# Gated delta rule in a hybrid backbone: k first, q and v loaded behind the block inverse's way to scratch, decayed queries made one step ahead

## The chip, the cores and the metric

One Trainium2 chip, one of its cores. The metric is the device time of one execution in microseconds (us); the median of the executions counts. A whole two-layer network runs in one program, and the change touches one of its stages, which occurs once in each layer.

## What is computed

The network has two layers; each is a feed-forward block, a token mixer, and a second feed-forward block, on 256 context and 256 latent tokens of width 1024. The mixer has four branches (a state space scan, an mLSTM, an S5 scan and a gated delta rule, GDN), whose outputs are gated and merged. The change is in the GDN branch. Cut to what matters (4 heads, keys and values of 128, run forward and backward over the tokens; the kernel uses chunks of 128 tokens where the reference has 64):

```python
def gdn_scan(q, k, v, lg, beta, s0):
    g = cumsum(lg) within a chunk
    lmat = (k*beta) k^T * exp(masked_diff(g, strict))
    tmat = triangular_solve(eye + lmat, eye)          # the inverse
    u_base, w_k = tmat (v*beta), tmat (k*beta*exp(g))
    a_qk = q k^T * exp(masked_diff(g))
    q_dec = q * exp(g)                                # decayed queries
    step: u = u_base - w_k s;  o = q_dec s + a_qk u;  s = exp(g_last) s + k_dec^T u
```

Before it q, k and v pass a short convolution and SiLU, and q and k are normalized to unit length. In layer 0 all four chunks give outputs; in layer 1 only the two latent ones do (`o0 = 2` skips q and the outputs of the others).

## The kernel before

**Order of the work.** `Backbone.mix` (L1817) walks a list of words written out by hand, `MIX_ORDER` (L1752), one string for each layer. A word like `ga2` is a projection of the gates (a pair of weight chunks, 2 x 24 matmuls); `gdn:1` runs the generator `Gdn.gdn` to its next `yield`, `gdn:6` six yields; `glu`, `zG0`, `m1` are other projections; `out` takes the GDN result through its norm, and `m0` to `m3` merge the branches. The order of words is a priority: the scheduler of the language orders each engine's instructions at build time by its own model of times, and an instruction that it holds ready early goes ahead of earlier words. `"!"` in front of a word queues its instructions behind the latest projection's last matmul on PE, weight cast on ACT, weight split on DVE and weight load on SP; `"'"` behind the last matmul alone. The queue of each engine is then fixed, and each engine works it in order.

**Projections.** `weights` (L360) loads a 512 KB chunk on the SP queue (L365), casts it on ACT (L366) and splits off the low part on DVE (L371); `proj` (L384) runs three matmuls for each product (L380 to L382). Three chunks are buffered (`nwf = 3`, L35). Small tiles (`k2`) come from a ring of 11 buffers (L33), big ones (`t8`) from ten numbered places.

**GDN** (L1234 on), by yields: (1) `to_tok` for k: four loads L1246, transposes L1249, copy L1250, squares L1253 and their sums L1254; (2) the same for v; (3) for q, then one `rsqrt` over both sums (L264 to L270), the normalization (L1267) and the transposes back (L1270, L1271); (4 to 7) for each chunk c the products k k^T (L1288) and k q^T (L1292), the decay E for both directions (loaded over all partitions, L1295; ACT L1298 for the forward one, GpSimd L1300 for the backward one, exponential L1301), the entries of the inverse's matrix LT on DVE (L1303), and the attention weights (L1306 on GpSimd, L1307 on DVE). Then `inverse`: the 32 x 32 diagonal blocks go to scratch in DRAM, one for each partition (BD L1134 and L1135, eight stores `gl` L1141, one load L1147), are solved by 31 substitution steps (L1158, L1160, columns below 12 on DVE and the rest on GpSimd), and come back (store `gz` L1162, eight loads L1168, transposes L1169); matmuls L1194 to L1225 double the blocks to 64 and 128. Four steps of the recurrence follow (L1321 to L1362); each makes its decayed queries in place (load L1350, exponential L1351, product L1352) ahead of the matmuls L1356.

Of the kernel before, what the change touches and what calls it, by code (L numbers as in the profile page):

```python
# [562 lines left out]
ORDER = ((0, 1, 2, 3), (1, 0, 3, 2))  # L563
# [555 lines left out]


class Gdn:
    def inverse(self, LT):


        nc = self.nc
        pt_ = nc.gpsimd.tensor_tensor
        sub = lambda: [self.k2([128, 16, 32]) for _ in range(2)]
        dma = nc.sync.dma_start
        TT = [self.t8(5, [128, 16, 128]), None]

        BD = sub()
        for b in range(4):
            q = slice(32 * b, 32 * b + 32)
            nc.vector.transpose(BD[0][q], LT[0][q, :, q])  # L1134
            nc.scalar.copy(BD[1][q], LT[1][q, :, q])  # L1135
        dl = self.dp.tile([128, 32, 32], F32, tag="gl", name=self.nm("gl"), bufs=1)
        dz = self.dp.tile([128, 32, 32], F32, tag="gz", name=self.nm("gz"), bufs=1)
        dv = lambda t, b, d: t[b * 32 + d * 16:b * 32 + d * 16 + 16].rearrange("u r c -> r u c")
        for b in range(4):
            for d in range(2):  # L1140
                dma(dv(dl, b, d), BD[d][32 * b:32 * b + 32])  # L1141
        LZ = self.t8(6, [128, 2, 32, 32])
        Lo, Z = LZ[:, 0], LZ[:, 1]
        nc.gpsimd.memset(Z, 0.0)
        nc.gpsimd.memset(Z.rearrange("p a b -> p (a b)")[:, ::33], 1.0)
        nc.gpsimd.memset(TT[0], 0.0)
        dma(Lo, dl)  # L1147
        yield
        for j in range(31):
            n = 31 - j  # L1150
# [8 lines left out]
                   Z[:, j, c0:c1].unsqueeze(1).to_broadcast([128, n, m]), op=OP.mult)  # L1159
                op(Z[:, j + 1:, c0:c1], Z[:, j + 1:, c0:c1], pr, op=OP.subtract)  # L1160
        yield
        dma(dz, Z)  # L1162
        TT[1] = self.t8(6, [128, 16, 128])
        nc.gpsimd.memset(TT[1], 0.0)
        ZB, ZT = sub(), sub()
        for d in range(2):
            for b in range(4):
                dma(ZB[d][32 * b:32 * b + 32], dv(dz, b, d))  # L1168
            nc.vector.transpose(ZT[d], ZB[d])  # L1169
        X = lambda d: (ZB if d == 0 else ZT)[d]  # L1170
        XT = lambda d: (ZT if d == 0 else ZB)[d]
# [3 lines left out]
        for d in range(2):  # L1175
            for b in range(4):
                q = slice(32 * b, 32 * b + 32)
# [27 lines left out]
        for d, a, qa, qb, _ in half:  # L1205

            pt = self.ps()
# [13 lines left out]
        for two in (quart[:2], quart[2:]):  # L1221
            pt = [self.ps() for _ in two]
# [11 lines left out]
    def gdn(self, l, P, G, o0):  # L1234
        nc, A = self.nc, self.A
        W = A["w_in"][l]
        t0 = o0 * 128
        tt, ts, stt = nc.vector.tensor_tensor, nc.vector.tensor_scalar, nc.vector.scalar_tensor_tensor

        kt, vt, qt = (self.t8(i, [128, 4, 4, 128]) for i in (4, 7, 6))  # L1240
        ss = self.keep("gss", [128, 2, 4, 4])

        def to_tok(j0, dst, c0, sums):
            for c in range(c0, 4):
                src = self.k2([128, 4, 128])
                nc.sync.dma_start(src, self.dG[j0:j0 + 4, :, c * 128:(c + 1) * 128].rearrange("h p t -> p h t"))  # L1246
                pt = self.ps()
                for h in range(4):
                    nc.tensor.transpose(pt[:, h * 128:(h + 1) * 128], src[:, h], self.ident)  # L1249
                nc.scalar.copy(dst[:, c].rearrange("p h e -> p (h e)"), pt)  # L1250
                if sums is not None:
                    sq = self.k2([128, 4, 128])
                    nc.scalar.activation(sq, dst[:, c], AF.Square)  # L1253
                    nc.vector.tensor_reduce(sums[:, c], sq, axis=mybir.AxisListType.X, op=OP.add)  # L1254
        to_tok(4, kt, 0, ss[:, 0])
        yield
        to_tok(8, vt, 0, None)
        yield
        if o0:
            nc.gpsimd.memset(ss[:, 1, 0:o0], 1.0)  # L1260
        to_tok(0, qt, o0, ss[:, 1])
        self.rsqrt(ss, ss, 1.0)
        ts(ss[:, 1], ss[:, 1], 128 ** -0.5, None, op0=OP.mult)
        kT, qT = self.t8(3), self.t8(0)
        for t, T_, sums, c0 in ((kt, kT, ss[:, 0], 0), (qt, qT, ss[:, 1], o0)):
            for c in range(c0, 4):
                tt(t[:, c], t[:, c], sums[:, c].unsqueeze(2).to_broadcast([128, 4, 128]), op=OP.mult)  # L1267
                pt = self.ps()
                for h in range(4):
                    nc.tensor.transpose(pt[:, h * 128:(h + 1) * 128], t[:, c, h], self.ident)  # L1270
                nc.scalar.copy(T_[:, :, c * 128:(c + 1) * 128], pt.rearrange("p (h t) -> p h t", h=4))  # L1271
        rv = self.rowd[16:24].rearrange("(d h) t -> d h t", d=2)
        b4 = lambda ap: ap.unsqueeze(2).to_broadcast([128, 4, 128])
        hv = lambda p: p.rearrange("p (h v) -> p h v", h=4)
# [5 lines left out]

        at = [self.t8(8 + i, [128, 4, 4, 128]) for i in range(2 - l)]
        own = lambda c, d: at[(c - o0) // 2][:, c % 2 * 2 + d]
        for c in range(4):
            yield
            sl = slice(c * 128, (c + 1) * 128)
            pg, pa = self.ps(), None
            for h in range(4):
                nc.tensor.matmul(pg[:, h * 128:(h + 1) * 128], lhsT=kT[:, h, sl], rhs=kT[:, h, sl], start=True, stop=True)  # L1288
            if c >= o0:
                pa = self.ps()  # L1290
                for h in range(4):
                    nc.tensor.matmul(hv(pa)[:, h], lhsT=kT[:, h, sl], rhs=qT[:, h, sl], start=True, stop=True)  # L1292
            for d in range(2):
                E = self.k2([128, 4, 128])
                nc.sync.dma_start(E, rv[d, :, c * 128:(c + 1) * 128].partition_broadcast(128))  # L1295
                for h in range(4):
                    if d == 0:
                        nc.scalar.activation(E[:, h], E[:, h], AF.Relu, scale=-1.0, bias=G8("g", c, d, h))  # L1298
                    else:
                        nc.gpsimd.tensor_scalar(E[:, h], E[:, h], G8("g", c, d, h), 0.0, op0=OP.subtract, op1=OP.min)  # L1300
                nc.scalar.activation(E, E, AF.Exp, scale=(-1.0, 1.0)[d])  # L1301
                for h in range(4):
                    stt(LT[d][:, c * 4 + h], pg[:, h * 128:(h + 1) * 128], G["beta"][:, c, d, h:h + 1], E[:, h],  # L1303
                        op0=OP.mult, op1=OP.mult)
                if pa is not None:
                    nc.gpsimd.tensor_tensor(own(c, d), E, self.tri[:, d].unsqueeze(1).to_broadcast([128, 4, 128]), op=OP.mult)  # L1306
                    tt(own(c, d), own(c, d), hv(pa), op=OP.mult)  # L1307
        TT = yield from self.inverse(LT)
        yield
        oT, gS = self.t8(1), self.t8(2)  # L1310
        S, seen = [None, None], set()
        for i in range(4):
            cs = [ORDER[d][i] for d in range(2)]
            sl = [slice(c * 128, (c + 1) * 128) for c in cs]
            both = range(2)
# [28 lines left out]
            for d in both:  # L1344
                c = cs[d]
                if c < o0:
                    continue
                if i:
                    gb = self.k2([128, 4, 128])
                    nc.sync.dma_start(gb, rv[d, :, c * 128:(c + 1) * 128].partition_broadcast(128))  # L1350
                    nc.scalar.activation(gb, gb, AF.Exp)  # L1351
                    nc.gpsimd.tensor_tensor(gb, gb, qT[:, :, sl[d]], op=OP.mult)  # L1352
# [34 lines left out]
class S5:  # L1387
# [364 lines left out]
MIX_ORDER = (  # L1752
# [7 lines left out]
)  # L1760


# [245 lines left out]
```

## Time and profile before

| | us |
|---|---|
| median of 3 runs | 2816.64 (2812.92 to 2817.88) |
| the profiled execution's own time | 2805.0 |
| its span, first to last instruction | 2803.3 |
| TensorE busy | 2687.4 (96%) |
| VectorE busy | 1729.0 (62%) |
| mean granted TensorE clock | 0.979 of full speed |

Times below are positions in the profiled span. The GDN stage of layer 0 lies between 877 and 1123 us, that of layer 1 between 2343 and 2560 us. Engines: PE is TensorE, DVE VectorE, ACT ScalarE, POOL GpSimd, SP the queue that issues the DMAs.

### The profile page before, as it was taken

What the parts mean: (1) busy time and instruction counts of PE and PEld (TensorE: products, weight loads), DVE (VectorE), ACT (ScalarE), POOL (GpSimd) and SP (SyncE); (2) the same over time, 40 slices, a digit from 0 to 9 for tenths busy, and PEclk for the clock granted to TensorE, in tenths of its full rate; (3) what the DMA queues carried; (4) which work ended last, traced back from release to release, by engine and by line L of the source; (5) the groups of instructions that cost most, each with busy time, mean ns of one, the idle gap of its engine ahead of it and who ended that gap; (6) DMA issues with size and microseconds to landing.
All of it is one profiled execution on the core that took longest, in us unless ns stands there. A gap on an engine that the chain in (4) does not pass through costs nothing.

```text
span 2803.3 us, 46292 instructions
## 1 busy us (share of the span) xinstructions
PE 2687.4 (96%) x17710; PEld 2258.2 (81%) x17710; DVE 1729.0 (62%) x3234; ACT 1114.1 (40%) x1711; POOL 748.3 (27%) x1129
## 2 busy tenths in 40 slices
PE   7999999999999998999999999999998999969999
PEld 5777669787878778897678897777987888969999
DVE  6654436578975575674333476654464997776665
ACT  4322224445464542252212353323354556623544
POOL 1433001394030322520000024330016951434100
PEclk9999999999999999999999999999999999979999
DMA  8444887755475562567662364444476558753564
GB/s 267 127 156 123 266 278 225 172 165 159 143 214 172 147 202 92 196 209 258 228 232 91 98 167 122 134 131 127 132 201 188 160 186 252 223 164 118 178 195 151
DMA packets 509820, 494.18 MB, mean 176 GB/s; under 512 B 79381, under 2 KB 437839, under 8 KB 508575
## 3 DMA queue, kind: packets, MB, share of 16 engines
q1 hardware_dynamic: 509598, 491.22, 57.6%
q8 instruction: 140, 2.29, 0.3%
q14 instruction: 82, 0.66, 0.1%
HBM read 429.17 MB, written 61.96 MB: 175 GB/s over the span
## 4 chain that ended last, share of the span: by engine, by line
PE 50%; DVE 9%; issue 4%; DMA 4%; POOL 2%; ACT 1%; SPq 1%; DVEq 0%; POOLq 0%; ACTq 0%
PE ffn.pb L380 11%; PE ffn.pb L381 11%; PE ffn.pb L382 11%; PE gates.pb L380 2%; PE gates.pb L381 2%; PE gates.pb L382 2%; PE ffn.ps L187 1%; PE merge.pb L382 1%; PE merge.pb L380 1%; PE merge.pb L381 1%; DVE gdnin.kf L790 1%; PE wout.pb L382 1%; PE wout.pb L381 1%; PE wout.pb L380 1%; DVE ssmin.kf L790 1%
## 5 line engine op out<-in xcount | busy, mean ns | idle before, releaser
L371 DVE TENSOR_TENSOR ffn.wl<-ffn.wf,ffn.wh 128x1024 fp32r<-128x1024 f32 (+1 forms) x308 | 369.3, 1199 | 373.1 <-ACT ffn.wh L366 363.6
L366 ACT CAST ffn.wh<-ffn.wf 128x1024 fp32r<-128x1024 f32 (+1 forms) x308 | 310.7, 1009 | 550.9 <-PE ffn.pb L382 388.3
L382 PE MATMUL ffn.pb<-ffn.t,ffn.wh 128*128 128x256 f32 (+1 forms) x1312 | 437.5, 336 | 0.0
L381 PE MATMUL ffn.pb<-ffn.t,ffn.wl 128*128 128x256 f32 (+1 forms) x1312 | 437.3, 335 | 0.0
L380 PE MATMUL ffn.pb<-ffn.t,ffn.wh 128*128 128x256 f32 (+1 forms) x1312 | 433.7, 337 | 1.0 <-ACT ffn.t L344 1.0
L380 PEld LDWEIGHTS ffn.pb<-ffn.t,ffn.wh 128*128 128x128 f32 x1312 | 243.4, 188 | 34.2 <-ACT ffn.wh L366 4.2
L382 PEld LDWEIGHTS ffn.pb<-ffn.t,ffn.wh 128*128 128x128 f32 x1312 | 246.3, 188 | 30.0 <-issue 2.4
L381 PEld LDWEIGHTS ffn.pb<-ffn.t,ffn.wl 128*128 128x128 f32 x1312 | 247.2, 188 | 28.3 <-issue 1.6
L380 PE MATMUL ffn.pb<-wout.t,ffn.wh 128*128 128x256 f32 (+1 forms) x720 | 240.8, 336 | 1.0 <-ACT wout.t L344 1.0
L381 PE MATMUL ffn.pb<-wout.t,ffn.wl 128*128 128x256 f32 (+1 forms) x720 | 239.6, 333 | 0.0
L382 PE MATMUL ffn.pb<-wout.t,ffn.wh 128*128 128x256 f32 (+1 forms) x720 | 237.3, 332 | 0.0
L381 PE MATMUL gates.pb<-ffn.t,gates.wl 128*128 128x512 f32 (+1 forms) x512 | 176.7, 346 | 5.4 <-DVE gates.wl L371 5.4
L313 POOL TENSOR_TENSOR norm.kf<-norm.kf,norm.kf 128x256 f32<-128x256 f32 x45 | 43.0, 956 | 518.0 <-ACT norm.kf L311 517.3
L380 PE MATMUL gates.pb<-ffn.t,gates.wh 128*128 128x512 f32 (+1 forms) x512 | 175.2, 344 | 0.6 <-ACT zs.kf L807 0.6
L382 PE MATMUL gates.pb<-ffn.t,gates.wh 128*128 128x512 f32 (+1 forms) x512 | 175.8, 344 | 0.0
L380 PEld LDWEIGHTS ffn.pb<-wout.t,ffn.wh 128*128 128x128 f32 x720 | 135.9, 189 | 26.6 <-ACT ffn.wh L366 7.5
L381 PEld LDWEIGHTS ffn.pb<-wout.t,ffn.wl 128*128 128x128 f32 x720 | 136.1, 189 | 16.2 <-DVE ffn.kf L498 0.8
L382 PEld LDWEIGHTS ffn.pb<-wout.t,ffn.wh 128*128 128x128 f32 x720 | 134.9, 188 | 15.9 <-issue 0.8
L380 PE MATMUL ffn.pb<-t,ffn.wh 128*128 128x512 f32 x352 | 141.9, 404 | 2.0 <-DVE ffn.kf L493 1.9
L381 PE MATMUL ffn.pb<-t,ffn.wl 128*128 128x512 f32 x352 | 142.3, 405 | 0.0
L382 PE MATMUL ffn.pb<-t,ffn.wh 128*128 128x512 f32 x352 | 138.9, 400 | 0.0
L493 DVE SCALAR_TENSOR_TENSOR ffn.kf<-ffn.kf,ffn.pb 128x512 f32<-128x512 f32 (+1 forms) x88 | 54.6, 620 | 94.8 <-ACT ffn.kf L491 94.8
(583 smaller groups left out, 6321.0 us busy)
## 6 DMA issues: line engine op xcount, KB each, us to landing
ffn.wf<-in_ffn_up_dram SPq DMA_DIRECT2D x176, 512.0 KB
ffn.t<-in_ada_w_dram SPq DMA_DIRECT2D x68, 1024.0 KB
ffn.wf<-in_ffn_down_dram SPq DMA_DIRECT2D x104, 512.0 KB
gates.wf<-in_w_in_dram SPq DMA_DIRECT2D x64, 512.0 KB
merge.wf<-in_w_branch_dram SPq DMA_DIRECT2D x32, 512.0 KB
zs.wf<-in_w_in_dram SPq DMA_DIRECT2D x24, 512.0 KB
gdnin.wf<-in_w_in_dram SPq DMA_DIRECT2D x24, 512.0 KB
wout.wf<-in_w_out_dram SPq DMA_DIRECT2D x24, 512.0 KB
```

Of the source, the lines that this page charges most:

```text
L187: nc.tensor.matmul(pm[32 * k:32 * k + 32, :], lhsT=self.sF[:, h * 4 + k, 28 - 4 * i:60 - 4 * i], rhs=ws[h][:, k], start=(h == 0), stop=(h ...
L313: nc.gpsimd.tensor_tensor(sq[0], sq[0], q, op=OP.add)
L366: self.w_cast = nc.scalar.copy(wh[:, :nk, :nw], wf[:, :nk, :nw])
L371: self.w_split = nc.vector.tensor_tensor(wl[:, :nk, :nw], wf[:, :nk, :nw], wh[:, :nk, :nw].bitcast(F32), op=OP.subtract)
L380: mm(out, lhsT=ah, rhs=bh, start=start, stop=False)
L381: mm(out, lhsT=al, rhs=bh, start=False, stop=False)
L382: self.last_mm = mm(out, lhsT=ah, rhs=bl, start=False, stop=stop)
L493: nc.vector.scalar_tensor_tensor(g[:, :n], t[:, :n], 1.0, p, op0=OP.add, op1=OP.mult)
L790: nc.vector.scalar_tensor_tensor(av, tap(k), cw[:, k:k + 1], av, op0=OP.mult, op1=OP.add)
```

## The change

K is loaded and normalized first, by itself. The decay rows are loaded one chunk ahead, and the backward decay is made on DVE rather than on GpSimd. The diagonal blocks go to scratch in two parts (the first 12 of the 16 chunk-head pairs after chunk 2, the last four after chunk 3), each part with one DMA for each direction over all 128 partitions, in a scratch laid out as direction, pair, row. Q is loaded and normalized behind the blocks' way to scratch, and the attention weights are finished there; v is loaded behind the substitution and transposed (`values`) while the blocks come back, which takes two loads instead of eight. The inverse's tile is in place 7 instead of 6, where v comes later. The decayed queries are made one step ahead. The words of `MIX_ORDER` are respaced. The core of the diff, with `...` for what is left out:

```diff
-    def inverse(self, LT):
+    def inverse(self, LT, values):
...
+        for u in (slice(0, 12), slice(12, 16)):
+            for b in range(4):
+                q = slice(32 * b, 32 * b + 32)
+                nc.vector.transpose(BD[0][q, u], LT[0][q, u, q])
+                nc.scalar.copy(BD[1][q, u], LT[1][q, u, q])
             for d in range(2):
-                dma(dv(dl, b, d), BD[d][32 * b:32 * b + 32])
-        LZ = self.t8(6, [128, 2, 32, 32])
+                dma(dl[d, u].rearrange("u q c -> q u c"), BD[d][:, u])
+            if u.start == 0:
+                yield
+        LZ = self.t8(7, [128, 2, 32, 32])
...
         for d in range(2):
-            for b in range(4):
-                dma(ZB[d][32 * b:32 * b + 32], dv(dz, b, d))
+            dma(ZB[d], dz[d].rearrange("u q c -> q u c"))
+        values()
+        for d in range(2):
             nc.vector.transpose(ZT[d], ZB[d])
...
-        to_tok(4, kt, 0, ss[:, 0])
-        yield
-        to_tok(8, vt, 0, None)
-        yield
...
+        def normalized(t, T_, sums, c0):
+            self.rsqrt(sums[:, c0:], sums[:, c0:], 1.0, 0)
...
+        src = load(4, 0)
+        yield
+        to_tok(src, kt, 0, ss[:, 0])
+        yield
+        kT = self.t8(3)
+        normalized(kt, kT, ss[:, 0], 0)
...
+        Es = rows(0)
         for c in range(4):
             yield
...
+            Ec, Es = Es, rows(c + 1) if c < 3 else None
...
-                        nc.gpsimd.tensor_scalar(E[:, h], E[:, h], G8("g", c, d, h), 0.0, op0=OP.subtract, op1=OP.min)
+                        ts(E[:, h], E[:, h], G8("g", c, d, h), 0.0, op0=OP.subtract, op1=OP.min)
...
+            if c > 1:
+                next(inv)
+        src = load(0, o0)
+        yield
+        qt, qT = self.t8(6, [128, 4, 4, 128]), self.t8(0)
+        to_tok(src, qt, o0, ss[:, 1])
+        normalized(qt, qT, ss[:, 1], o0)
...
+        yield
+        next(inv)
+        v["src"] = load(8, 0)
+        yield
+        TT = yield from inv
...
         for i in range(4):
+            for d in range(2) if i < 3 else ():
+                c = ORDER[d][i + 1]
+                if c >= o0:
+                    gb = gbs[i + 1, d] = self.k2([128, 4, 128])
+                    nc.sync.dma_start(gb, rv[d, :, c * 128:(c + 1) * 128].partition_broadcast(128))
+                    nc.scalar.activation(gb, gb, AF.Exp)
+                    nc.gpsimd.tensor_tensor(gb, gb, qT[:, :, c * 128:(c + 1) * 128], op=OP.mult)
...
-    "!s5:1 ga2 's5:1 gb2 s5:1 gdn:1 gc2 gdn:1 gd2 gdn:6 ga0 glu gb0 gc0 gd0 zG0 zG2 !gdn:1 ga3 gb3 'gdn:6 gc3 gd3 "
-    "out m1 m2 m3 m0",
+    "!s5:1 ga2 's5:1 gb2 s5:1 gdn:1 gc2 gdn:1 glu gdn:2 gd2 gdn:1 ga0 gdn:1 gb0 gdn:1 gc0 gdn:1 gd0 !gdn:1 zG0 zG2 "
+    "ga3 gb3 !gdn:1 gc3 'gdn:6 gd3 out m1 m2 m3 m0",
...
-    "'ssm:1 i4 !ssm:1 i6 !ssm:1 i8 !ssm:1 i10 !ssm:1 i0 !ssm:1 !s5:1 i2 's5:1 zG0 s5:1 zG2 gdn:1 ga2 gdn:1 gb2 gdn:6 "
-    "gc2 glu gd2 ga1 gb1 gc1 gd1 ga0 gb0 gc0 gd0 !gdn:1 ga3 gb3 'gdn:6 gc3 gd3 out m2 m1 m3 m0",
+    "'ssm:1 i4 !ssm:1 i6 !ssm:1 i8 !ssm:1 i10 !ssm:1 i0 !ssm:1 !s5:1 i2 's5:1 zG0 s5:1 zG2 gdn:1 ga2 gdn:1 gb2 glu "
+    "gdn:2 gc2 gdn:1 gd2 gdn:1 ga1 gdn:1 gb1 gdn:1 gc1 gd1 !gdn:1 ga0 gb0 gc0 gd0 ga3 gb3 !gdn:1 gc3 'gdn:6 gd3 out "
+    "m2 m1 m3 m0",
```

## Rows read from the trace of the kernel before

**Rows 1.** The page: busy us, share of the span, instructions; then 40 slices in tenths.
```profile
PE 2687.4 (96%) x17710; PEld 2258.2 (81%) x17710; DVE 1729.0 (62%) x3234; ACT 1114.1 (40%) x1711; POOL 748.3 (27%) x1129
...
PE   7999999999999998999999999999998999969999
```

**Rows 2.** Stretches: length, busy us (xcount) of PE, PEld, DVE, ACT, POOL; clock, DMA.
```profile
2343.00:2482.40 139.40, 127.08 (x1062) 124.27 (x1061) 109.09 (x218) 84.59 (x143) 48.41 (x65) 0.98 0.84 246
2482.40:2498.80 16.40, 0.00 (x0) 0.00 (x0) 11.07 (x32) 1.04 (x1) 6.62 (x6) 0.56 0.56 175
2498.80:2524.20 25.40, 22.51 (x448) 22.01 (x448) 10.71 (x22) 8.46 (x14) 5.11 (x7) 0.54 0.12 19
2524.20:2559.80 35.60, 31.91 (x259) 31.06 (x257) 18.61 (x54) 7.58 (x15) 10.01 (x9) 0.95 0.16 45
877.80:975.90 98.10, 94.43 (x464) 77.31 (x462) 52.51 (x78) 51.91 (x87) 26.82 (x27) 1.00 0.58 172
```

**Rows 3.** Timeline of PE, layer 1: start, us, instruction, [idle before <- what ended it].
```profile
2377.62 0.55 PE L1249 MATMUL gdn.ps<-ident,gdn.k 128*128 128x128 f32 x3 [1.20 <-DMA gdn.k<-ffn.gdn]
...
2427.54 0.58 PE L381 MATMUL gates.pb<-ffn.t,gates.wl 128*128 128x256 f32 x1 [4.08 <-DVE gates.wl L371]
...
2454.37 0.28 PE L380 MATMUL merge.pb<-ffn.t,merge.wh 128*128 128x256 f32 x1
...
2498.83 1.38 PE L1194 MATMUL gdn.ps<-gdn.k,gdn.t 32*32 32x32 f32 x22 [16.46 <-DMA gdn.k<-gdn.gz]
...
2504.79 3.27 PE L1194 MATMUL gdn.ps<-gdn.k,gdn.t 32*32 32x32 f32 x61 [2.53 <-DVE gdn.k L1169]
...
2552.62 1.95 PE L283 MATMUL gdn.ps<-ones,gdn.k 128*128 128x1 f32 x16 [1.29 <-ACT gdn.k L839]
2556.57 3.47 PE L300 MATMUL gdn.ps<-ident,gdn.rstd 128*128 128x128 f32 x16 [2.00 <-POOL gdn.rstd L258]
```

**Rows 4.** Timeline of DVE, layer 1, from k's last sum to the end of the substitution.
```profile
2372.64 0.69 DVE L1254 TENSOR_REDUCE gdn.gss<-gdn.k 128x4 f32<-128x512 f32 x1
...
2390.98 0.18 DVE L264 TENSOR_SCALAR gdn.rsq<-gdn.gss 128x32 f32<-128x32 f32 x1
...
2425.08 1.27 DVE L1307 TENSOR_TENSOR gdn.t<-gdn.t,gdn.ps 128x512 f32<-128x512 f32 x2
...
2442.87 0.21 DVE L1158 TENSOR_TENSOR gdn.gpr<-gdn.t 128x31 f32<-128x31 f32 x1 [1.95 <-DMA gdn.t<-gdn.gl]
...
2494.05 0.17 DVE L1160 TENSOR_TENSOR gdn.t<-gdn.t,gdn.gpr 128x12 f32<-128x12 f32 x1
```

**Rows 5.** Timeline of the SP queue, layer 1: the GDN's loads among others.
```profile
2371.84 4.69 SPq L1246 DMA_DIRECT2D gdn.k<-ffn.gdn  x5
...
2388.78 7.67 SPq L1295 DMA_DIRECT2D gdn.k<-rows.rowd  x8
...
2435.97 0.47 SPq L1147 DMA_DIRECT2D gdn.t<-gdn.gl  x1
```

**Rows 6.** Groups, layer 1: xcount | busy us, mean ns of one | idle before <- releasers.
```profile
L1300 POOL TENSOR_SCALAR gdn.k<-gdn.k,rows.gc 128x128 f32<-128x128 f32 x16 | 16.8, 1068 | 54.8 <-ACT gdn.k L1298 54.8
...
L371 DVE TENSOR_TENSOR merge.wl<-merge.wf,merge.wh 128x1024 fp32r<-128x1024 f32 x9 | 12.1, 1346 | 1.7 <-ACT merge.wh L366 1.7
L818 DVE TENSOR_SCALAR gates.kf<-gates.kf 128x256 f32<-128x256 f32 x30 | 11.8, 396 | 7.5 <-ACT gates.kf L817 7.5
...
L1160 DVE TENSOR_TENSOR gdn.t<-gdn.t,gdn.gpr 128x192 f32<-128x192 f32 (+16 forms) x18 | 7.0, 389 | 0.2
```

**Rows 7.** Timelines of PE and ACT, layer 0.
```profile
975.89 2.08 PE L1288 MATMUL gdn.ps<-gdn.t 128*128 128x128 f32 x8 [2.61 <-DVE gdn.t L1303]
...
1051.72 2.01 PE L1194 MATMUL gdn.ps<-gdn.k,gdn.t 32*32 32x32 f32 x61
...
1110.76 0.63 ACT L1351 ACTIVATE gdn.k<-gdn.k 128x512 f32<-128x512 f32 x1 [5.95 <-DMA gdn.k<-rows.rowd]
...
1112.78 0.80 PE L1356 MATMUL gdn.ps<-gdn.k,gdn.t 128*128 128x128 f32 x2 [4.44 <-POOL gdn.k L1352]
```

More of the change, by code (lines that the diff above doesn't have):

```diff
@@ L1128, in inverse @@
         dma = nc.sync.dma_start
-        TT = [self.t8(5, [128, 16, 128]), None]
+        dl, dz = (self.dp.tile([2, 16, 128, 32], F32, tag=n, name=self.nm(n), bufs=1) for n in ("gl", "gz"))
         BD = sub()
-        for b in range(4):
[L1133 to L1139, printed above, removed]
+        for u in (slice(0, 12), slice(12, 16)):
[3 more added lines that the diff above has]
+                nc.scalar.copy(BD[1][q, u], LT[1][q, u, q])
             for d in range(2):
-                dma(dv(dl, b, d), BD[d][32 * b:32 * b + 32])
-        LZ = self.t8(6, [128, 2, 32, 32])
+                dma(dl[d, u].rearrange("u q c -> q u c"), BD[d][:, u])
+            if u.start == 0:
+                yield
+        LZ = self.t8(7, [128, 2, 32, 32])
         Lo, Z = LZ[:, 0], LZ[:, 1]
@@ L1145, in inverse @@
         nc.gpsimd.memset(Z.rearrange("p a b -> p (a b)")[:, ::33], 1.0)
+        TT = [self.t8(5, [128, 16, 128]), None]
         nc.gpsimd.memset(TT[0], 0.0)
-        dma(Lo, dl)
+        dma(Lo, dl.rearrange("d u (b r) c -> (d u b) r c", b=4))
         yield
@@ L1161, in inverse @@
         yield
-        dma(dz, Z)
+        dma(dz.rearrange("d u (b r) c -> (d u b) r c", b=4), Z)
         TT[1] = self.t8(6, [128, 16, 128])
@@ L1166, in inverse @@
         for d in range(2):
-            for b in range(4):
-                dma(ZB[d][32 * b:32 * b + 32], dv(dz, b, d))
+            dma(ZB[d], dz[d].rearrange("u q c -> q u c"))
+        values()
+        for d in range(2):
             nc.vector.transpose(ZT[d], ZB[d])
@@ L1238, in gdn, with load, to_tok @@
         tt, ts, stt = nc.vector.tensor_tensor, nc.vector.tensor_scalar, nc.vector.scalar_tensor_tensor
-        kt, vt, qt = (self.t8(i, [128, 4, 4, 128]) for i in (4, 7, 6))
+        kt = self.t8(4, [128, 4, 4, 128])
         ss = self.keep("gss", [128, 2, 4, 4])
[L1243 to L1246, printed above, removed]
+        def load(j0, c0):
+            src = [self.k2([128, 4, 128]) for _ in range(c0, 4)]
+            for s, c in zip(src, range(c0, 4)):
+                nc.sync.dma_start(s, self.dG[j0:j0 + 4, :, c * 128:(c + 1) * 128].rearrange("h p t -> p h t"))
+            return src
+        def to_tok(src, dst, c0, sums):
+            for s, c in zip(src, range(c0, 4)):
                 pt = self.ps()
                 for h in range(4):
-                    nc.tensor.transpose(pt[:, h * 128:(h + 1) * 128], src[:, h], self.ident)
+                    nc.tensor.transpose(pt[:, h * 128:(h + 1) * 128], s[:, h], self.ident)
                 nc.scalar.copy(dst[:, c].rearrange("p h e -> p (h e)"), pt)
@@ L1254, in to_tok @@
                     nc.vector.tensor_reduce(sums[:, c], sq, axis=mybir.AxisListType.X, op=OP.add)
-        to_tok(4, kt, 0, ss[:, 0])
-        yield
-        to_tok(8, vt, 0, None)
-        yield
[L1259 to L1265, printed above, removed]
+        def normalized(t, T_, sums, c0):
+            self.rsqrt(sums[:, c0:], sums[:, c0:], 1.0, 0)
+            if t is not kt:
+                ts(sums[:, c0:], sums[:, c0:], 128 ** -0.5, None, op0=OP.mult)
             for c in range(c0, 4):
@@ L1282, in gdn, with values, rows @@
         own = lambda c, d: at[(c - o0) // 2][:, c % 2 * 2 + d]
+        v = {}
+        def values():
+            v["t"] = self.t8(7, [128, 4, 4, 128])
+            to_tok(v["src"], v["t"], 0, None)
+        inv = self.inverse(LT, values)
+        def rows(c):
+            E = [self.k2([128, 4, 128]) for _ in range(2)]
+            for d in range(2):
+                nc.sync.dma_start(E[d], rv[d, :, c * 128:(c + 1) * 128].partition_broadcast(128))
+            return E
+        Es = rows(0)
         for c in range(4):
@@ L1285, in gdn @@
             sl = slice(c * 128, (c + 1) * 128)
-            pg, pa = self.ps(), None
+            pg = self.ps()
             for h in range(4):
                 nc.tensor.matmul(pg[:, h * 128:(h + 1) * 128], lhsT=kT[:, h, sl], rhs=kT[:, h, sl], start=True, stop=True)
[L1289 to L1292, printed above, removed]
+            Ec, Es = Es, rows(c + 1) if c < 3 else None
             for d in range(2):
-                E = self.k2([128, 4, 128])
-                nc.sync.dma_start(E, rv[d, :, c * 128:(c + 1) * 128].partition_broadcast(128))
+                E = Ec[d]
                 for h in range(4):
@@ L1304, in gdn @@
                         op0=OP.mult, op1=OP.mult)
-                if pa is not None:
+                if c >= o0:
                     nc.gpsimd.tensor_tensor(own(c, d), E, self.tri[:, d].unsqueeze(1).to_broadcast([128, 4, 128]), op=OP.mult)
-                    tt(own(c, d), own(c, d), hv(pa), op=OP.mult)
-        TT = yield from self.inverse(LT)
+            if c > 1:
[5 more added lines that the diff above has]
+        normalized(qt, qT, ss[:, 1], o0)
+        for c in range(o0, 4):
+            sl = slice(c * 128, (c + 1) * 128)
+            pa = self.ps()
+            for h in range(4):
+                nc.tensor.matmul(hv(pa)[:, h], lhsT=kT[:, h, sl], rhs=qT[:, h, sl], start=True, stop=True)
+            for d in range(2):
+                tt(own(c, d), own(c, d), hv(pa), op=OP.mult)
+        yield
[3 more added lines that the diff above has]
+        TT = yield from inv
+        vt = v["t"]
         yield
@@ L1311, in gdn @@
         S, seen = [None, None], set()
+        gbs = {}
         for i in range(4):
+            for d in range(2) if i < 3 else ():
+                c = ORDER[d][i + 1]
+                if c >= o0:
+                    gb = gbs[i + 1, d] = self.k2([128, 4, 128])
+                    nc.sync.dma_start(gb, rv[d, :, c * 128:(c + 1) * 128].partition_broadcast(128))
+                    nc.scalar.activation(gb, gb, AF.Exp)
+                    nc.gpsimd.tensor_tensor(gb, gb, qT[:, :, c * 128:(c + 1) * 128], op=OP.mult)
             cs = [ORDER[d][i] for d in range(2)]
@@ L1347, in gdn @@
                     continue
[L1348 to L1352, printed above, removed]
+                gb = gbs.pop((i, d), None)
                 po = self.ps()
```

## The prediction

> **What bounds the kernel now.** The page first: TensorE is busy 96% of the span [rows 1], so outside its gaps nothing on another engine shortens the kernel, and 116 us of gaps (2803.3 less 2687.4) are all that a reordering can win, apart from matmuls that run at a lower clock. The slices show one deep hole, a 6 at the 36th [rows 1], which is layer 1's GDN stage. So the second view is that of stretches there [rows 2]: from 2343 to 2482 PE is busy 127.1 of 139.4 us, with gates, the first merges and the GDN's preparation; then it does nothing for 16.4 us; then come the inverse's matmuls (25.4 us, granted clock 0.54, thus mostly at the lower of the two levels, 1.2 GHz) and the recurrence (35.6 us). The third view, PE's timeline, names what ended each gap [rows 3]: the 16.46 us wait for the solved blocks to come back from scratch, and 2.53 us more for the other direction's transposes. All that PE could do beside the GDN was done by then, since the next merge (m3) needs the GDN's output. The chain behind that wait is read on DVE [rows 4]: k's sums are ready at 2373.3, yet its norm starts only at 2391.0, when q's sums are there too; the last attention weights end at 2426.3; the substitution starts at 2442.9, when the blocks have come through scratch, and ends at 2494.2.
>
> In layer 0 the gaps are small: 2.61 us behind the entries of LT, and 4.44 us behind decayed queries, whose load kept ACT waiting 5.95 us [rows 7].
>
> **Part by part, layer 1.** *K first.* The norm of k no longer waits for v and q: 2391.0 less 2373.3 is 17.7 us off the chain. What v and q cost there (six of the ten loads, transposes, copies) isn't saved, only moved: q stands behind the blocks' way to scratch, v behind the substitution. PE has gates to run at both places.
>
> *The chunks.* The four attention products L1307 leave the chain (two of them took 1.27 us [rows 4], so 2.5 us). The backward decay goes from GpSimd, where 16 instructions took 16.8 us [rows 6], to DVE. No row shows this one on DVE; the nearest is a tensor_scalar of twice the width, 396 ns [rows 6]; below it stands the 0.18 us of one of 32 columns [rows 4]. I take 0.29, the middle: 16 of them are 4.6 us of DVE (2.9 to 6.3). So this stretch is longer by 2 us. The Trainium skill (GPSIMD Engine Reference, section 4.1 Engine selection) says that GpSimd does one-input elementwise work at roughly the Vector engine's rate, which speaks against this move: by it DVE would get all 16.8 us. No run here shows the operation on DVE.
>
> *To scratch in two parts.* From 2425 to 2442.9 the blocks took 18 us: transposes, eight stores, one load, which was issued at 2435.97 [rows 5] and landed 6.9 us later. Three quarters now go a chunk earlier, and two stores follow instead of eight. Transposes and stores should shrink by 4 us of the 10 ahead of that load; 0 to 6 are the ends.
>
> Together the substitution would start at 2442.9 - 17.7 + 2 - 4 = 2423. Of its 31 steps, 18 had started within the 39.5 us to 2482.4 [rows 6], and 13 took the 12 us after that, with little beside them. It now runs beside gates alone, not merges; I take 35 to 45 us, so it ends at 2458 to 2468, some 30 us earlier. What it is queued behind (the splits of d1, for the way back those of b3) is done before that, since in this profile all gates are through PE when the first merge starts at 2454.4 [rows 3]. The work that PE had left from there (merges m2 and m1, to 2482) now covers the rest: the blocks are back at about 2463 to 2473. So the **16.46 us** go, and the **2.53** with them (two loads instead of eight). If the substitution kept its 51 us, 2423 + 51 + 5 = 2479 would still be in time; with no gain from the smaller edits and gates that drag, 8 us of the wait would stay.
>
> *Clock.* The 61 small matmuls that took 3.27 us behind the gap [rows 3] took 2.01 us in layer 0 [rows 7], where no such gap lay ahead. On 192 such matmuls (128 of L1194, 64 of L1201) that is 192/61 x 1.26 = **4.0 us**; without the gap PE has been busy, and the clock should stay. Ends: 0 and 4.
>
> *The tail.* PE waits 1.29 and 2.00 us for the output's norm [rows 3]. If merges are left they fill it; half, **1.6 us** (0 to 3.3).
>
> *What it costs.* DVE gets 4.6 us of decay, a second `rsqrt` (12 instructions at 0.18, 2.2 us), and four short transposes (1 us): 7.8 us. In 2343 to 2482 it was busy 109.1 of 139.4 us, 11.1 more followed in the gap [rows 2]; of these, the 12.1 us of the merges' splits [rows 6] may come later, and some of their products with them. What must be done by 2463 is thus at most 109 + 11 + 8 - 12 = 116 us in 120, nine tenths or more. When DVE worked through the chunks before, PE stood 4.08 us for a weight split [rows 3]; I charge one and a half of that, **6 us** (0 to 12). On SP the four loads of k, q and v now come in a row; a row of five took 4.69 us there and eight rows of decay 7.67 [rows 5], behind the first PE stood 1.20 us [rows 3]. Three weight chunks of 24 matmuls are buffered ahead, at 139.4/1062 us a matmul [rows 2] 9 us of work, which hides these; without that cover they would cost their issue times.
>
> *Decayed queries ahead.* In layer 1 they were not the last wait; nothing. The ring of 11 small tiles then holds four of them at a time, two more than before, beside r, U and the decayed keys (six).
>
> Sum, layer 1: 16.5 + 2.5 + 4.0 + 1.6 - 6.0 = 18.6 us.
>
> **Layer 0.** The 4.44 us go, as the queries are loaded a step earlier, over ten microseconds ahead against 5.95 of waiting. Of the 2.61, where GpSimd's decay had held the chunk back, half: 1.3. DVE's 8 us more are hidden: it is busy 52.5 of 98.1 us there while PE is full [rows 2]. Sum 5.7 us (4.4 to 7.1).
>
> Together 24.3 us. The profiled execution would come to 2805.0 - 24.3 = 2780.7; it ran 11.6 us under the median of the runs, and on their scale that is 2816.6 - 24.3 = **2792.3 us**.
>
> **Rivals.** *DVE becomes the bound.* If it is full from the chunks to the end of the substitution, the splits come late, the gates stretch, and what was one gap comes back as many. Price: 12 us for the gates and 2 for the tail that isn't covered, so 24.3 - 6 - 2 - a wait for the blocks of 5 leaves 11, or 2805. For it: the nine tenths above; against it: DVE has only 29 us of work in the 61 after the blocks return [rows 2]. The Trainium skill's rule on one-input work (GPSIMD Engine Reference, section 4.1 Engine selection) would put 16.8 rather than 4.6 us on DVE and lead here.
>
> *SP held by the ring of small tiles (slower).* Loads now ask for four tiles at a time; v's are held across the way back, where four tiles for the blocks and two more are asked for as well, ten of 11. Should SP wait at one of these for a free tile, all weight loads behind it wait, and PE starves once 9 us of buffered chunks are used. Held for 28 us in each layer it costs 2 x 19, which gives 2816.6 - 24.3 + 38 = 2830; it decides from 24 us a layer on (2 x 15 = 30 against the 24.3 won and the 5.6 of a margin). For it: v's transposes must pass a PE queue full of merges before the tiles come free. Against: the longest burst here held SP 7.67 us [rows 5].
>
> *The wait stays.* The order is fixed at build time by a model. If it puts q's work ahead of the last chunk after all, or the way back behind the merges on some queue, the blocks come back after PE has run dry as before: a second 16 us gap, and the small gains are eaten by DVE's new work: 2816.
>
> **Chances.** Forecast 0.60; DVE bound 0.17; the wait stays 0.12; SP held 0.11. A measurement tells about 0.2% (5.6 us) from no change. Faster takes the first and nearly all of the second, 0.76; within 0.2% the third and a rest, 0.13; slower 0.11. The range: below, all terms at their good ends (16.5 + 2.5 + 4.0 + 3.3, the 4.1 of the late split, the 1.2 behind loads, layer 0 at 7.1: 38.7) give 2778, and 3 us for the spread of the runs 2775; above, it takes in the second and the third rival, 2818.
>
> **What would show it.** Right: no gap over 3 us ahead of L1194 in layer 1; k's norm right behind its sums; the substitution starting near 2423 and ending before the last gates and merges; clock at or near 1 through L1194 to L1225; merges among the inverse's matmuls; in layer 0 no wait of L1356 on the decayed queries. Wrong: a new gap of over 8 us on PE whose releaser is a load on SP or a weight split; DVE over nine tenths busy through the gates with PE below it; a single decay instruction on DVE near 1 us.

## The result, and the profile after

The changed kernel is **faster**: 2779.77 us, median of four runs (2778.71 to 2790.5), against 2817.26 for the kernel before on the same chip; ratio 0.9887 on record, 95% interval 0.9866 to 0.9908. The medians lie 37.5 us apart, the ratio makes it 32 us. Measured twice more beside the experiments it gave 0.9918 (0.9903 to 0.9932) and 0.9888 (0.9868 to 0.9909). The profiled executions differ by 26.3 us: 2805.0 before, 2778.71 after.

The page of the changed kernel (busy us, share of the span, instructions; then slices in tenths) answers to [rows 1]; the 6 in the 36th slice is gone, and PE's idle time fell from 116 to 86 us (2776.9 less 2691.1):

```profile
PE 2691.1 (97%) x17710; PEld 2261.6 (81%) x17710; DVE 1731.2 (62%) x3298; ACT 1112.9 (40%) x1719; POOL 721.1 (26%) x1096
...
PE   7999999999999999999999999999998998999999
```

Where it was won is read from matching matmuls: the SSM's last one ahead of the GDN's stage, and the first of the output projection.

| us in the span | before | after | gained between |
|---|---|---|---|
| layer 0: last SSM matmul | 850.4 | 856.5 | -6.1 (ahead of all changes) |
| first of the output projection | 1195.4 | 1187.9 | 13.5 |
| layer 1: last SSM matmul | 2337.5 | 2325.6 | 4.5 |
| first of the output projection | 2581.6 | 2553.4 | 16.4 |
| end | 2803.3 | 2776.9 | -1.9 |

The rows ahead of the first stage, between the stages and behind the second hold none of the changed work; their -6.1, 4.5 and -1.9 us show how far two executions differ by themselves. In the two further profiles of the changed kernel the two stages gained 10.8 and 13.8, and 11.0 and 20.2 us.

Stretches of both stages, with the columns of [rows 2], the kernel before first:

```profile
878.00:1195.40 317.40, 305.41 (x1893) 256.78 (x1892) 198.60 (x355) 118.91 (x182) 102.68 (x108) 0.97 0.55 167
2309.00:2588.90 279.90, 241.29 (x2348) 234.81 (x2347) 204.33 (x422) 137.18 (x226) 100.62 (x112) 0.90 0.64 191
```

and the same work in the changed kernel:

```profile
884.10:1187.90 303.80, 301.43 (x1892) 253.56 (x1891) 196.15 (x387) 117.79 (x186) 89.13 (x89) 0.98 0.56 171
2300.60:2560.20 259.60, 241.23 (x2349) 234.18 (x2347) 208.18 (x453) 136.19 (x229) 84.96 (x96) 0.94 0.70 205
2330.00:2450.40 120.40, 110.10 (x888) 107.06 (x884) 103.78 (x254) 74.71 (x136) 29.70 (x45) 0.94 0.85 240
```

In layer 1 PE's idle time fell by 20.2 us (38.6 to 18.4) and its busy time not at all; in layer 0 by 9.6 (12.0 to 2.4), and the busy time by 4.0. PE's timeline in layer 1 shows the place; answers to [rows 3]:

```profile
2339.08 0.63 PE L1256 MATMUL gdn.ps<-ident,gdn.k 128*128 128x128 f32 x4 [3.17 <-DMA gdn.k<-ffn.gdn]
...
2450.53 2.08 PE L1196 MATMUL gdn.ps<-gdn.k,gdn.t 32*32 32x32 f32 x64 [0.37 <-DMA gdn.k<-gdn.gz]
...
2522.72 1.95 PE L283 MATMUL gdn.ps<-ones,gdn.k 128*128 128x1 f32 x16 [1.29 <-ACT gdn.k L839]
...
2526.65 3.57 PE L300 MATMUL gdn.ps<-ident,gdn.rstd 128*128 128x128 f32 x15 [1.99 <-POOL gdn.rstd L258]
```

The inverse waits 0.37 us where it waited 16.46. The chain behind it, on DVE (answers to [rows 4]), with the norm right behind k's last sum:

```profile
2345.88 0.69 DVE L1261 TENSOR_REDUCE gdn.gss<-gdn.k 128x4 f32<-128x512 f32 x1 [0.26 <-ACT gdn.k L1260]
2346.60 0.17 DVE L264 TENSOR_SCALAR gdn.rsq<-gdn.gss 128x16 f32<-128x16 f32 x1
...
2394.25 0.31 DVE L1159 TENSOR_TENSOR gdn.gpr<-gdn.t 128x31 f32<-128x31 f32 x1
...
2440.58 0.17 DVE L1161 TENSOR_TENSOR gdn.t<-gdn.t,gdn.gpr 128x12 f32<-128x12 f32 x1
```

and on the SP queue: k's four loads at once, q's two, the way back:

```profile
2334.80 2.30 SPq L1249 DMA_DIRECT2D gdn.k<-ffn.gdn  x4
...
2369.61 1.06 SPq L1249 DMA_DIRECT2D gdn.k<-ffn.gdn  x2
...
2440.83 0.32 SPq L1163 DMA_DIRECT2D gdn.gz<-gdn.t  x1
2446.11 2.04 SPq L1168 DMA_DIRECT2D gdn.k<-gdn.gz  x2
```

### The profile page after: what moved, and what is told of

Read it like the earlier page. It is cut to its first block, busy times and chain, and to the rows that moved or that the text cites. A ratio compares the mean times of both kernels' runs of the same rounds, so it can differ in the third digit from the quotient of the medians.

```text
span 2776.9 us, 46285 instructions
## 1 busy us (share of the span) xinstructions
PE 2691.1 (97%) x17710; PEld 2261.6 (81%) x17710; DVE 1731.2 (62%) x3298; ACT 1112.9 (40%) x1719; POOL 721.1 (26%) x1096
## 4 chain that ended last, share of the span: by engine, by line
PE 56%; DVE 7%; issue 3%; DMA 3%; POOL 1%; ACT 1%; SPq 0%; DVEq 0%; POOLq 0%; ACTq 0%
PE ffn.pb L380 11%; PE ffn.pb L382 11%; PE ffn.pb L381 11%; PE gates.pb L380 2%; PE gates.pb L381 2%; PE gates.pb L382 2%; PE merge.pb L381 1%; PE ffn.ps L187 1%; PE merge.pb L380 1%; PE merge.pb L382 1%; DVE gdnin.kf L790 1%; PE wout.pb L382 1%; PE wout.pb L381 1%; PE wout.pb L380 1%; POOL merge.t L1844 1%
## 5 line engine op out<-in xcount | busy, mean ns | idle before, releaser
L381 PEld LDWEIGHTS gates.pb<-ffn.t,gates.wl 128*128 128x128 f32 x512 | 99.1, 194 | 18.7 <-DVE gates.wl L371 7.1
```

Of the source, the lines that this page charges most:

```text
L381: mm(out, lhsT=al, rhs=bh, start=False, stop=False)
```

## The experiments

Each kernel ran beside the kernel before on the same chip, in three sets; ratios are to the kernel before of the set. The changed kernel itself stands in the second and the third set; the four of the first set are compared with it by their ratios.

| | median us | ratio, 95% interval |
|---|---|---|
| *first set, before 2814.13* | | |
| queries in place | 2788.07 | 0.9912 (0.9895 to 0.9929) |
| decay on GpSimd | 2786.96 | 0.9914 (0.9897 to 0.9931) |
| scratch in one part | 2778.74 | 0.9889 (0.9869 to 0.9909) |
| q and v ahead | 2794.87 | 0.9938 (0.9921 to 0.9955) |
| *second set, before 2808.86* | | |
| m0 ahead | 2777.49 | 0.9894 (0.9872 to 0.9916) |
| old words | 2773.71 | 0.9876 (0.9863 to 0.9888) |
| the changed kernel | 2786.37 | 0.9918 (0.9903 to 0.9932) |
| before, queries ahead | 2802.60 | 0.9976 (0.9961 to 0.9991) |
| *third set, before 2810.04* | | |
| K first alone | 2779.18 | 0.9893 (0.9875 to 0.9911) |
| old words, m0 ahead | 2781.29 | 0.9892 (0.9870 to 0.9914) |
| the same, one part | 2776.84 | 0.9879 (0.9860 to 0.9899) |
| the changed kernel | 2777.40 | 0.9888 (0.9868 to 0.9909) |

### One part undone: q and v ahead

```diff
...
         to_tok(src, kt, 0, ss[:, 0])
...
+        to_tok(load(8, 0), vt, 0, None)
+        to_tok(load(0, o0), qt, o0, ss[:, 1])
         yield
...
+        normalized(qt, qT, ss[:, 1], o0)
         normalized(kt, kT, ss[:, 0], 0)
...
```

> The changed kernel with one part undone: v and q are loaded and transposed, and q is normalized, ahead of the chunks again, right behind k's transposes (the attention products stay behind the blocks' way to scratch; the tile of the inverse is in place 6 again, since v holds place 7). Theory A (the order of loads is what freed the chain): k's norm waits for v and q again, the substitution in layer 1 starts 10 to 18 us later than 2394, PE waits for the blocks ahead of the inverse's first matmuls for 8 to 16 us, and the time is 2788 to 2796. Theory B (the respaced words and the smaller edits brought the gain, and PE's cover is large enough either way): no gap over 3 us ahead of the inverse and a time within 4 us of 2779.8.

Theory A's time and its chain are met: 0.9938, at the far end of all runs with the change, and the substitution starts 14.9 us later than in the changed kernel, counted from k's first load (74.4 us behind it against 59.5); 12.4 us of that is the norm, which waits for v and q again. The wait isn't where A put it. DVE's first step of the substitution, then PE's two largest gaps in layer 1 and the one ahead of the inverse:

```profile
2416.83 0.21 DVE L1159 TENSOR_TENSOR gdn.gpr<-gdn.t 128x31 f32<-128x31 f32 x1 [1.38 <-DMA gdn.t<-gdn.gl]
```

```profile
2377.76 0.58 PE L381 MATMUL gates.pb<-ffn.t,gates.wl 128*128 128x256 f32 x1 [5.24 <-DVE gates.wl L371]
...
2413.23 0.58 PE L381 MATMUL gates.pb<-ffn.t,gates.wl 128*128 128x256 f32 x1 [5.50 <-DVE gates.wl L371]
...
2467.38 1.79 PE L1196 MATMUL gdn.ps<-gdn.k,gdn.t 32*32 32x32 f32 x54 [1.82 <-DMA gdn.k<-gdn.gz]
```

The blocks cost PE 1.82 us only, for two reasons: PE itself comes later, and the substitution took 38.9 us instead of 46.5. PE comes later because it waited 5.24 and 5.50 us for splits of weights. The first of these stood in DVE's queue behind decay instructions that waited for their own rows, the second behind the GDN's chunk work, in which DVE had no pause. DVE ahead of the first:

```profile
2375.69 0.88 DVE L1319 TENSOR_SCALAR gdn.k<-gdn.k,rows.gc 128x128 f32<-128x128 f32 x4 [1.53 <-DMA gdn.k<-rows.rowd]
2376.48 1.22 DVE L371 TENSOR_TENSOR gates.wl<-gates.wf,gates.wh 128x1024 fp32r<-128x1024 f32 x1
```

Of the stretches in the table above, layer 0 gained 3.2 us and layer 1 9.8, together 13.0 against 24.6 to 31.2 in the changed kernel's three profiles. So with q and v back in front, two fifths to a half of the gain stays.

### K first by itself

The changed kernel with the words of before, queries in place, decay on GpSimd and one part to scratch (the diffs of the sections below together).

> The new order of loads (k first, q behind the blocks' way to scratch, v behind the substitution) nearly by itself: the words spaced as before the change, the decayed queries in place, the backward decay on GpSimd, the blocks to scratch in one part. What remains of the change beside the order of loads: two loads of the blocks back instead of eight, and the decay rows loaded a chunk ahead. Theory A (the order of loads frees layer 1's chain, worth some 14 us by the run with q and v ahead; the queries are worth 6): layer 1's wait ahead of the inverse is under 4 us, the queries' gaps of 3 to 4.5 us are back, and the time is 14 to 22 us below the kernel before, a ratio of 0.992 to 0.995. Theory B (the parts are needed together, above all the shorter chunks and the early scratch): the wait is still over 8 us and the ratio is 0.996 or more.

Theory A, and more than it expected: 0.9893 beside 0.9888 for the whole change. Layer 0 gained 11.0 and layer 1 19.8 us. The inverse's waits, then the queries', on PE:

```profile
2473.07 2.08 PE L1194 MATMUL gdn.ps<-gdn.k,gdn.t 32*32 32x32 f32 x64 [0.99 <-DMA gdn.k<-gdn.gz]
...
2476.46 1.78 PE L1194 MATMUL gdn.ps<-gdn.k,gdn.t 32*32 32x32 f32 x31 [1.31 <-DVE gdn.k L1169]
```

```profile
1101.89 0.49 PE L1392 MATMUL gdn.ps<-gdn.k,gdn.t 128*128 128x128 f32 x2 [1.69 <-POOL gdn.k L1388]
```

The queries' wait in layer 0 shrinks from 4.44 to 1.69 with nothing done about the queries, where theory A had it back at 3 to 4.5; in layer 1 there is none, as before.

Where the chain of layer 1 got shorter, in us counted from the issue of k's first load (the last column has the matmuls of the merges that stand ahead of the inverse on PE):

| | k's sums ready | norm's wait | norm to substitution | in all | PE's wait for the blocks | merges ahead |
|---|---|---|---|---|---|---|
| before | 29.6 | 17.7 | 51.9 | 99.1 | 16.46 | 192 |
| K first alone | 16.1 | 0 | 65.5 | 81.6 | 0.99 | 192 |
| old words | 15.1 | 2.3 | 61.9 | 79.3 | 2.90 | 192 |
| q and v ahead | 12.2 | 12.4 | 49.8 | 74.4 | 1.82 | 0 |
| the changed kernel | 11.8 | 0 | 47.7 | 59.5 | 0.37 | 2 |

In its two further profiles the changed kernel has 59.9 and 59.6. K first alone makes the chain 17.5 us shorter, as much as the norm had waited (the sums come 13.5 us earlier, and the stretch behind the norm takes 13.6 longer), and that is enough to end the long wait for the blocks. The respaced words take 20 us more off the chain, but they also put the inverse ahead of the merges, so PE needs the blocks that much sooner, and the time gains nothing that these runs show. What came with the new order in this run (k's loads issued at once, two loads back instead of eight, the decay rows a chunk ahead) wasn't tried apart from it.

### The decayed queries, both ways

Put back in place in the changed kernel, and moved ahead in the kernel before (the reverse):

```diff
-            for d in range(2) if i < 3 else ():
...
-                gb = gbs.pop((i, d), None)
+                if i:
+                    gb = self.k2([128, 4, 128])
...
```

> The changed kernel with one part undone: the decayed queries are loaded, exponentiated and multiplied in the step that uses them, as before the change, in both layers. Theory A (layer 0's gain is this wait, 4.44 us, with the clock and the small gaps around it): PE waits again for the decayed queries in layer 0's recurrence, one gap of 3 to 5 us there, and the time rises by 3 to 6 us over the changed kernel's 2779.8, to 2783 to 2786. Theory B (layer 0's gain comes from the respaced words, which leave merges and gates between the recurrence's steps): what is left between the steps covers the wait, no gap over 1 us ahead of the queries' matmuls, and the time stays within 2 us of 2780. Layer 1 should not change by either.

> The kernel before with one part of the change alone: the decayed queries are made one step ahead in the recurrence. Theory A (the prediction's terms): layer 0's gap of 4.44 us ahead of the queries' matmuls goes, layer 1 gains nothing, as the queries were not its last wait; 4 to 6 us faster than the kernel before, a ratio of 0.998 to 0.9986. Theory B (the wait moves to the next late thing, the entries of r or the state, or the two loads more in SP's queue hold a weight load): less than 2 us, a ratio of 0.9993 or more.

In place, PE's gaps are these, in layer 0 as A had it and, by neither theory, in layer 1:

```profile
1103.47 0.49 PE L1394 MATMUL gdn.ps<-gdn.k,gdn.t 128*128 128x128 f32 x2 [3.27 <-POOL gdn.k L1390]
...
2512.44 0.80 PE L1394 MATMUL gdn.ps<-gdn.k,gdn.t 128*128 128x128 f32 x2 [3.61 <-POOL gdn.k L1390]
```

The time, 0.9912, lies between the changed kernel's own measurements, so the two gaps are shown and their price isn't. Ahead in the kernel before, the move is worth 6.3 us by the medians (ratio 0.9976), theory A; its profile gained 7.0 us in layer 0, and layer 1's wait of the inverse stood unmoved:

```profile
2495.04 2.15 PE L1194 MATMUL gdn.ps<-gdn.k,gdn.t 32*32 32x32 f32 x40 [17.91 <-DMA gdn.k<-gdn.gz]
```

### The decay on GpSimd, and scratch in one part

```diff
-                        ts(E[:, h], E[:, h], G8("g", c, d, h), 0.0, op0=OP.subtract, op1=OP.min)
+                        nc.gpsimd.tensor_scalar(E[:, h], E[:, h], G8("g", c, d, h), 0.0, op0=OP.subtract, op1=OP.min)
```

> The changed kernel with one part undone: the backward decay (32 instructions of 128 x 128 in the two layers) runs on GpSimd again instead of on VectorE, where one took 0.28 us. One should take about 1.07 us, as in the kernel before (1068 ns). Theory A (GpSimd does a chunk's four in 4.3 us and keeps pace with the chunks, which come 4 to 5 us apart; K first carries the change): the substitution in layer 1 starts within 3 us of the changed kernel's 2394 and the time stays within 3 us of 2779.8. Theory B (the move to VectorE shortens the chain, and the inverse stands in PE's order with only 0.37 us to spare): the chain is 8 to 12 us later, PE waits that long ahead of the inverse, and the time is 2788 to 2792.

```diff
-        for u in (slice(0, 12), slice(12, 16)):
+        for u in (slice(0, 16),):
...
-            if c > 1:
+            if c > 2:
                 next(inv)
```

> The changed kernel with one part undone: all 16 diagonal blocks go to scratch after the last chunk, in two stores (one for each direction), not three quarters of them a chunk earlier. Theory A: four transposes of 512 columns stand where four of 128 stood (0.30 us each against about 0.75), so the substitution starts 2 us later, and PE, which has 0.37 us to spare ahead of the inverse in layer 1, waits 0 to 2 us more; the time is 2780 to 2783. Theory B (the early part is what makes the chain short, as the 4 us of the prediction): the chain is 4 to 6 us later, PE waits as much, and the time is 2784 to 2787.

Groups of the decay in layer 1 (count, busy us, mean ns), in the changed kernel and on GpSimd:

```profile
L1317 DVE TENSOR_SCALAR gdn.k<-gdn.k,rows.gc 128x128 f32<-128x128 f32 x16 | 3.6, 279 | 0.0
```

```profile
L1318 POOL TENSOR_SCALAR gdn.k<-gdn.k,rows.gc 128x128 f32<-128x128 f32 x16 | 14.6, 931 | 18.9 <-DMA gdn.k<-rows.rowd 18.9
```

On GpSimd the substitution started at 2397.32, 59.1 us behind k's first load, no later than in the changed kernel (59.5 to 59.9). The 2787 us look like a loss of 7, but the changed kernel itself gave 2786.37 in the next set, and K first alone, which has this decay too, 0.9893; a price of the decay isn't shown. In one part, the substitution started 61.5 us behind k's first load, 2 us later, as theory A had it; PE didn't wait for the blocks, and the time is the changed kernel's: the early part buys chain that nobody waits for.

### The words, and m0 ahead

```diff
-    "gdn:2 gc2 gdn:1 gd2 gdn:1 ga1 gdn:1 gb1 gdn:1 gc1 gd1 !gdn:1 ga0 gb0 gc0 gd0 ga3 gb3 !gdn:1 gc3 'gdn:6 gd3 out "
+    ... gdn:6 gc2 glu gd2 ga1 gb1 gc1 gd1 ga0 gb0 gc0 gd0 !gdn:1 ga3 gb3 !gdn:1 'gdn:6 gc3 gd3 out ...
```

These are layer 1's words; layer 0's go back likewise.

> The changed kernel with its words spaced as before the change (the GDN's steps bunched in front of the gates as they were; the new steps that the change makes beside them). In layer 1 all 192 merges then stand ahead of the inverse on PE. Theory A (K first freed the chain): the blocks are back well before the merges end, no wait over 1 us ahead of the inverse; but nothing is left to run beside the inverse and the recurrence, whose gaps come back (6.6 us between 2498.8 and 2559.8 before the change), so it is 4 to 9 us above the changed kernel's time on the same chip. Theory B (the respaced words brought the gain): PE waits 8 us or more for the blocks again and the time is 12 to 20 us above.

Both theories missed. PE waits 2.90 us ahead of the inverse, so K first holds, but the time isn't above the changed kernel's; it is 12.7 us below it in that set.

```profile
2471.94 2.56 PE L1196 MATMUL gdn.ps<-gdn.k,gdn.t 32*32 32x32 f32 x64 [2.90 <-DMA gdn.k<-gdn.gz]
```

Against the changed kernel's 0.9887 and 0.9888 in the other sets, 0.9876 is no difference. So the spacing is worth nothing in time that these runs show, and may cost, though it makes the chain 20 us shorter.

```diff
-    "m2 m1 m3 m0",
+    "m2 m1 m0 m3",
```

> The changed kernel with the last two words of layer 1's order exchanged: merge m0, which needs nothing of the GDN, goes ahead of m3, which needs its output. In the changed kernel the merges ran out at 2501.4, and of the 28.7 us to the first matmul of m3 PE was idle 4.8 us (gaps of 1.31, 1.29 and 1.99 among them), at a granted clock of 0.84. Theory A (the recurrence's tail lacks cover): m0's 96 matmuls more than fill the gaps of the recurrence, the clock stays up there, and the time falls by 3 to 7 us below the changed kernel's. Theory B (the tail is a chain of its own, which m0's splits and matmuls lengthen, and what isn't left for the end is missed there, since the chain of m3 to the output then stands last): no gain or a loss, within 2 us of it or up to 5 us above.

> Two edits of the changed kernel together: the words spaced as before the change, and layer 1's merge m0 ahead of m3. With the old words alone the recurrence of layer 1 had no merges left beside it: between 2485 and 2530 PE was idle 3.6 us at a granted clock of 0.84, and stood 2.90 us ahead of the inverse. Theory A (cover is missing there, and m0's 96 matmuls give it): those gaps shrink and the clock stays up, 3 to 6 us faster than the old words alone (ratio to the kernel before 0.9876), so 0.9855 to 0.9866. Theory B (the tail that follows, m3 and the output projection with no other merge beside them, gives it back, as when m0 went ahead by itself, whose recurrence ended later): within 2 us, 0.987 to 0.9885.

> The same two edits (words spaced as before the change, m0 ahead of m3) with a third: the blocks go to scratch in one part, with two stores instead of four. Theory A (the early part is worth nothing; two stores and eight instructions less free SP and VectorE a little): the same as without it, within 3 us. Theory B (with the old words the blocks come back 2.90 us later than PE is ready, so a chain 2 us longer shows in full): 2 to 4 us slower than without it.

With m0 ahead by itself the gap of 1.31 in the recurrence went, but those of 1.29 and 1.99 at the output's norm stayed in all three: the build hands m0's matmuls to the recurrence before them, and none are left for the norm. By itself it gave 2777.5 beside 2786.4, with the old words 2781.3 beside 2777.4, and there its ratio, 0.9892, lies above both theories' ranges: no effect that holds. One part instead of two gave 4.5 us less by the medians, outside theory A's 3 us, but the intervals overlap; of theory B's loss there is no sign. No version is shown to beat the changed kernel, which alone was measured in more than one set.

### The changed kernel again

> The changed kernel itself, unaltered, as a measure for the experiments: 2779.8 us on record, with single executions from 2778.7 to 2790.5. Expected 2778 to 2784 and a ratio to the kernel before of 0.9866 to 0.9908.

> The changed kernel itself once more, as the measure for the three runs beside it: a ratio to the kernel before between 0.9887 and 0.9918, the two measured so far, and single executions that lie in two groups, near 2779 and near 2788, according to whether the clock stays at the lower level through the inverse's matmuls in layer 1 (20 us of it in a profile of 2788.2, 4 us in one of 2778.7).

The first of these lay above its range, 2786.37; the third at its lower end. Two groups of times can't be told apart among 15 executions (2771.7 to 2793.8). What the profile of 2788.2 shows is told at the end.

## Why the prediction was right

The profiled execution was to come to 2780.7 us and took 2778.71; on the scale of the medians 2792.3 against 2779.8, since the profile of before ran 11.6 us under its median and that of after 1 us. The mechanism is the one forecast: k's norm no longer waits for q and v, the blocks are back in time, and PE's long wait is gone. Its terms:

- **The wait for the blocks**, 16.46 + 2.53: gone but for 0.37, 18.6 us. Right.
- **The chain**: forecast to start the substitution at 2423 and end it at 2458 to 2468; measured 2394.25 and 2440.75. K's first load was issued 8.9 us earlier than before, so that is 20 and at least 8 us ahead of the forecast. The failed step is "k's sums are ready at 2373.3", taken from before: there k's four loads were issued one by one between other transfers (the lines below), and the sums came 29.6 us behind the first; now the four go at once, and the sums are there at 2346.57, 11.8 us behind the first. The words had no term at all: with the old ones the stretch from the norm to the substitution takes 61.9 us, not 47.7. The substitution took 46.5 us, more than the 35 to 45.

```profile
2343.73 0.48 SPq L1246 DMA_DIRECT2D gdn.k<-ffn.gdn  x1
...
2363.27 0.46 SPq L1246 DMA_DIRECT2D gdn.k<-ffn.gdn  x1
```

- **DVE**: the decay was put at 0.29 us for each instruction and takes 0.279. "Nine tenths or more" was a little high: 103.8 of 120.4 us, 86%; over the whole stage DVE got 3.9 us more to do (208.2 less 204.3), not 7.8. The charge of **6 us** for it didn't come: all idle time other than the wait fell by 1.6 us (20.2 less 18.6).
- **Clock**, 4.0, and **tail**, 1.6: neither came. PE's busy time in layer 1 is the same, though the first 64 matmuls of the inverse took 2.08 us at full clock: the lower level stands elsewhere now, beside the gaps behind k's loads (0.91 over 2330 to 2390) and in the recurrence. The sign "clock at or near 1" through the inverse wasn't met (0.88 over 2463.9 to 2478.5 here, 0.54 over the same matmuls in the second profile, last section). The tail's gaps are 1.29 and 1.99.
- **Layer 0**, 5.7: measured 10.8 to 13.5 in three profiles. The failed step is that the order of loads was given only half of 2.61 there, as what the decay on GpSimd had cost. K first alone, with the decay still on GpSimd, has neither that gap nor the queries' full one, and brought 11.0 us: the inverse comes earlier, 75 matmuls of the gates run beside it and the recurrence where there were none before, so the queries' wait shrinks by itself. The queries alone brought 7.0, and both together hardly more than the first: the terms overlap and were added.

So layer 1 (13.8 to 20.2 in three profiles, forecast 18.6) was right by the wait and, for the rest, by luck: errors that cancel, 6 not paid against 5.6 not won. Layer 0 was undersized by half. Of the rivals, SP was not held: its longest row of GDN loads took 8.74 us, and in the three profiles no load of a small tile ahead of the recurrence waited 2 us. It had been held longer in the kernel before than the prediction read: 31.0 us, to 2532.00, at a load of the decayed queries in layer 1. The wait didn't stay, and DVE didn't become the bound in the changed kernel; the run with q and v ahead comes nearest to that case, with splits that PE waited over 5 us for.

The Trainium skill (GPSIMD Engine Reference, section 4.1 Engine selection) was weighed with its statement that one-input elementwise work runs on GpSimd at roughly the Vector engine's rate. The traces differ: 931 ns on GpSimd against 279 on VectorE for the same instruction. By the rule DVE would have got 14.6 us in layer 1; it got 4.5. All these instructions are 128 columns wide; no run here varies the width, so how much of the 931 ns is a cost for each instruction stays open.

## What to carry to other kernels

Where an engine stands for a round trip, read its chain back to the first step that waits for something it doesn't use; here one norm shared by q and k held k for 17.7 us, and k's own loads, issued one by one between other transfers, held it for as much again. Moving the side branch behind the chain's own waits, nearly by itself, brought the whole gain; the finer edits that came with it couldn't be told from nothing. A chain that is made shorter than the work beside it wins no more: the respaced words took 20 us off it for no time. Don't add terms which the same cover can pay: a wait that has its own cure also shrinks when the work around it moves.

## What was unexpected in the hardware

The granted clock stayed at the lower level on a PE that the profile shows busy without a pause. In the changed kernel's second profile (2788.2 us) and in the first (2778.7), the same matmuls of the inverse, with merges between them, on the columns of [rows 2]:

```profile
2469.60:2491.10 21.50, 21.50 (x286) 20.35 (x280) 6.81 (x10) 4.79 (x8) 1.04 (x1) 0.54 0.39 124
2474.00:2490.00 16.00, 16.00 (x170) 15.03 (x170) 4.83 (x7) 2.42 (x4) 0.00 (x0) 0.50 0.20 60
```

```profile
2463.90:2478.50 14.60, 14.60 (x290) 13.90 (x286) 7.40 (x12) 4.33 (x7) 1.30 (x1) 0.88 0.49 155
```

PE is busy throughout both executions' stretches, with no gap over 0.2 us since the inverse began, and yet the one ran at 1.2 GHz for 16 us and more and took 6.9 us longer. Ahead of it stood matmuls of 32 x 32. The same hole stands in the profiles with m0 ahead (2470 to 2491, clock 0.54) and with the decay on GpSimd (2467 to 2489, 0.56), again with PE busy throughout. Why one execution falls into it and another doesn't stays open.

The Trainium skill (TensorE: Matmul & The Clock Gate, Part 1) says that throttling is the default and activity releases it; no run here shows what counts as activity, but a PE without gaps was not enough.
